# Scan inside a TensorE-bound trunk: the exponential behind the cast, y's scaling and norm sums on GpSimd, decays stored by kind, and the partition sums directly in front of the next transposes

## The chip, the cores and the metric

One core of one Trainium2 chip. The metric is the time of one execution in microseconds of device time, the median of several runs. TensorE is called PE below, VectorE DVE, ScalarE ACT, GpSimd POOL and SyncE SP, as the profile does.

## The reference, cut to what matters

One layer of a hybrid encoder on 2048 frames of 1024 columns, in float32: a norm, one input projection, a short gated convolution beside a state-space scan with 16 heads in 2 groups, an output projection over both, and an MLP. The change lies in the scan and in what follows it:

```python
x_c = xs * dt                                 # per head, 64 columns
a_cum = cumsum(dt * a_head)                   # inside a chunk
decay = exp(a_cum[l] - a_cum[s])  for l >= s  # per head, l x s
scores = C @ B.T                              # l x s, per group
y_diag = (scores * decay) @ x_c
states = B.T @ (x_c * exp(a_cum[-1] - a_cum))
h = h * exp(a_cum[-1]) + states               # carried from chunk to chunk
y_off = (C @ h_before) * exp(a_cum)
y = y_diag + y_off + d_skip * xs
gated = rmsnorm(y * silu(z))                  # over the 512 columns of a group
x = x + concat(y_a, gated) @ w_out
h = rmsnorm(x, norm_mlp_w)                    # the MLP's input
```

## The kernel before, in words

Time is cut into four blocks b of 512 frames. Every wide product is three matmuls of 128x128 by 512 on pieces of the operands (hi by hi, lo by hi, hi by lo; L114 to L116, and L271 to L273 where the products are combined in groups of seven). The in-projection of the blocks goes first, then the out-projection, then the MLP.

The scan works in 32 chunks of 128 frames: b (4) by group g (2) by c (4). A chunk n consists of:

- `load` (L1395 and on): bc (B and C), xd (x), and dec, the running sums of its 8 heads' decays, read from the HBM tensor rd_d and spread over all 128 partitions (L1411); `load_rows`: eb, the exponentials of the same sums, from the other half of rd_d; `load_gate`: the gate, into y (L1441).
- `front`: on PE four transposes ptx of x, one of B and the product C x B into ptb (L1459 to L1463); on ACT the copy xtok of ptx (L1465) and the hi casts of the pieces btok and xde (L1447), on DVE their lo parts (L1448), smask (scores under the triangle), xdt (xtok x dt, in a buffer stmp, L1471) and xtok x dend (L1473). Then, a step later, the decays: eight Relus on ACT (L1479), one Exp of 128x1024 (L1480), four scalings of xd by ACT (L1482). A step later DVE multiplies dec by smask (L1484).
- `back`: on PE st (three matmuls, new state, from btok and xde), yo (four, C by the old state, L1500) and yd (eight, dec by xdt, L1503); on DVE the state, y's sum and its gate (L1525); on ACT the squares of y (L1528), on DVE their sums over the four column tiles (L1529, L1531) into ssq. Then on PE the partition sum pss (ones by ssq, L1534, two passes), ACT's Sqrt (L1536), the reciprocal (L1537), y times it (L1539) and y's store to yn_d (L1540).

`run` is a generator, and its steps are laid between the products of the projection. The first 16 chunks (`bufs` 1, in the trace from 460 to 950 us) run beside the second half of the in-projection, a step after every 12 matmuls. The last 16 (`bufs` 2, from 950 to 1260 us) run beside the out-projection: `Output.unit` computes one column tile of one block in 24 matmuls, and its hook takes one step in the middle and two at its end. A chunk's loads are issued one chunk ahead in the first half and two ahead in the second. The unit's result is added to xt and stored (x1 in the orders, x_d in the trace; L1704, L1705), and its square is added to facc, the norm sum of the MLP's input (`Output.square`, L1716 to L1719).

The order of each engine's instructions is fixed when the program is built: a scheduler with its own estimate of times takes the instructions that are ready, in each engine's queue, with the tiles' buffers as a bound; `behind(x)` (L100) makes it put what is inside after instruction x. All DMAs here are issued by SP, in order. A DMA into a buffer waits there until the buffer's last reader is done, and so does all that is queued behind it.

Of the kernel before, what the change touches and what calls it, by code (L numbers as in the profile page):

```python
# [11 lines left out]
F32 = mybir.dt.float32  # L12
F32R = mybir.dt.float32r
AF = mybir.ActivationFunctionType
# [25 lines left out]
def trunk(ctx: ExitStack, tc: tile.TileContext, x, x_tok, w_in, w_dt, w_out, w_up, w_down, cvec, hrow, out):  # L40
# [20 lines left out]
    wide = lambda n, k: [dram.tile([P, k, TH], F32, name=f"{n}_d{h}") for h in range(2)]  # L61
    xs_d, sz_d, ys_d, yn_d = wide("xs", 12), wide("sz", 8), wide("ys", 8), wide("yn", 8)
    dt_d = [dram.tile([P, 4, NC * 16], F32, name=f"dt_d{b}") for b in range(NB)]
    rd_d = [dram.tile([NC * 16, 2, P], F32, name=f"rd_d{b}") for b in range(NB)]
    NQ = NF // 2
    hid_d = [[dram.tile([P, 7, TB], F32, name=f"hid_d{h}_{q}") for q in range(NQ)] for h in range(2)]
    sums_d = {}
# [32 lines left out]
    def behind(before):  # L100
        return tc.issue_after(before) if before is not None else nullcontext()
# [318 lines left out]
    class Proj(Seven):  # L420
# [304 lines left out]
        def dt_part(self, b):  # L725

            t = self.dt_tiles[b % NBB]
            v, e, d, p = (t[:, 64 * i : 64 * i + 64] for i in range(4))
            ct = t[:, 256:384]
            rows = t[0:64, 384:640].rearrange("p (a l) -> p a l", a=2)  # L730
            pd = psum("tp", "pd", 2)
            parts = [(k, h) for k in range(KD) for t in self.parts(b, k) for h in t]
            for n, (k, h) in enumerate(parts):
                nc.tensor.matmul(
                    pd[0:32, :], self.wdt[:, k, :], h, start=(n == 0), stop=(n == len(parts) - 1)
                )
            dts = (self.tmp("dts") if self.h == 0 else self.e("dts", TB))[0:32]
            nc.scalar.copy(dts, pd[0:32, :])
            yield
            pt = psum("tp", "pt", 2)  # L740
            for c in range(NC):
                nc.tensor.transpose(pt[:, c * 32 : (c + 1) * 32], dts[:, c * L : (c + 1) * L], ident[0:32, 0:32])
            three = lambda a: a.rearrange("p (c h) -> p c h", c=NC)
            nc.vector.tensor_reduce(
                out=three(v),
                in_=pt[:, 0 : NC * 32].rearrange("p (c s h) -> p c h s", c=NC, s=2),
                axis=mybir.AxisListType.X,
                op=ALU.add,
            )
            bias = self.hb[:, 0:16].unsqueeze(1).to_broadcast([P, NC, 16])  # L750
            nc.vector.tensor_tensor(out=three(v), in0=three(v), in1=bias, op=ALU.add)
            nc.vector.scalar_tensor_tensor(out=e, in0=v, scalar=-1.0, in1=v, op0=ALU.mult, op1=ALU.max)
            nc.scalar.activation(e, e, AF.Exp, scale=-1.0)

            nc.vector.tensor_scalar(out=d, in0=e, scalar1=2.0, scalar2=None, op0=ALU.add)
            nc.vector.reciprocal(out=d, in_=d)
            nc.vector.tensor_tensor(out=e, in0=e, in1=d, op=ALU.mult)
            nc.vector.tensor_tensor(out=d, in0=e, in1=e, op=ALU.mult)
            nc.vector.tensor_scalar(out=p, in0=d, scalar1=1.0 / 17, scalar2=None, op0=ALU.mult)
            for n in (15, 13, 11, 9, 7, 5, 3):  # L760
                nc.vector.scalar_tensor_tensor(out=p, in0=p, scalar=1.0 / n, in1=d, op0=ALU.add, op1=ALU.mult)
            nc.vector.scalar_tensor_tensor(out=p, in0=p, scalar=1.0, in1=e, op0=ALU.add, op1=ALU.mult)
            nc.vector.tensor_scalar(out=v, in0=v, scalar1=0.0, scalar2=None, op0=ALU.max)
            nc.vector.scalar_tensor_tensor(out=v, in0=p, scalar=2.0, in1=v, op0=ALU.mult, op1=ALU.add)
            nc.vector.tensor_tensor(
                out=three(e), in0=three(v), in1=self.a_neg.unsqueeze(1).to_broadcast([P, NC, 16]), op=ALU.mult
            )
            for _ in range(3 + 2 * self.h):
                yield
            pc = psum("tp", "pc", 2)  # L770
            nc.tensor.matmul(pc[:, 0:64], tri, e, start=True, stop=True)
            nc.tensor.matmul(pc[:, 64:128], ones, e, start=True, stop=True)
            nc.vector.tensor_copy(ct, pc[:, 0:128])
            nc.scalar.activation(p, ct[:, 64:128], AF.Exp)
            nc.vector.tensor_tensor(out=d, in0=ct[:, 64:128], in1=ct[:, 0:64], op=ALU.subtract)
            nc.scalar.activation(d, d, AF.Exp)
            nc.vector.tensor_tensor(out=d, in0=d, in1=v, op=ALU.mult)
            yield
            pr = psum("tp", "pr", 2)
            nc.tensor.transpose(pr[0:64, 0:P], ct[:, 0:64], ident)  # L780
            nc.vector.tensor_copy(rows[:, 0, :], pr[0:64, 0:P])
            nc.scalar.activation(rows[:, 1, :], pr[0:64, 0:P], AF.Exp)
            nc.sync.dma_start(rd_d[b], rows)
            for i, q in enumerate((v, ct[:, 0:64], p, d)):
                nc.sync.dma_start(dt_d[b][:, i], q)
            for _ in range(1 + self.h):
                yield
# [584 lines left out]
    class Scan:  # L1372
# [21 lines left out]
        def load(self, n):  # L1394

            if n >= self.end:
                return
            b, g, c, h, ts, r0 = self.place(n)
            t = self.got[n] = {}
            if (g, c) == (0, 0) or n == self.begin:  # L1400
                dd = self.tile([4, NC * 16], "dd")
                nc.sync.dma_start(dd, dt_d[b])
                self.dd = {**getattr(self, "dd", {}), b: dd}
            t["dd"] = dd = self.dd[b]
            bc = t["bc"] = self.tile([2, L], "bc", 2)
            for i in range(2):
                nc.sync.dma_start(bc[:, i], xs_d[h][:, 8 + 2 * i + g, ts])
            t["xd"] = self.tile([4, L], "xd")
            nc.sync.dma_start(t["xd"], xs_d[h][:, 4 * g : 4 * g + 4, ts])
            t["dec"] = self.tile([HG, L], "dec")  # L1410
            nc.sync.dma_start(t["dec"], rd_d[b][r0 : r0 + HG, 0, :].partition_broadcast(P))  # L1411
            three = lambda i: dd[:, i].rearrange("p (c h) -> p c h", c=NC)[:, c, g * HG : (g + 1) * HG]
            heads = lambda a: a.unsqueeze(2).to_broadcast([P, HG, 64])
            t["dt"], t["cdec"], t["dend"] = heads(three(0)), heads(three(2)), heads(three(3))
            t["a"] = dd[:, 1, r0 : r0 + HG]
            t["first"], t["last"] = (b, c) == (0, 0), (b, c) == (NB - 1, NC - 1)

        def load_rows(self, n):
# [11 lines left out]
                eb = eb[:, 0].rearrange("p (j l) -> p j l", j=4)  # L1430
            self.got[n]["eb"] = eb
            for hf in range(2):
                src = rd_d[b][r0 : r0 + HG, 1, :].rearrange("(j t) l -> t j l", t=2)[hf]
                nc.sync.dma_start(eb[hf * 64 : (hf + 1) * 64], src.partition_broadcast(64))

        def load_gate(self, n):
# [6 lines left out]
        def pieces(self, shape, tag, src):  # L1443

            pair = self.sp.tile([P] + shape, F32R, tag=tag, name=tag, bufs=1)
            hi, lo = pair[:, 0], pair[:, 1]
            nc.scalar.copy(hi, src)  # L1447
            nc.vector.tensor_tensor(out=lo, in0=src, in1=hi.bitcast(F32), op=ALU.subtract)  # L1448
            return hi, lo

        def front(self, n):
# [20 lines left out]
            if not t["last"]:  # L1472
                nc.vector.tensor_tensor(out=byhead(xtok), in0=byhead(xtok), in1=t["dend"], op=ALU.mult)  # L1473
                t["xde"] = self.pieces([2, 512], "xde", xtok)
            yield

            dec = t["dec"]
            for i in range(HG):
                nc.scalar.activation(dec[:, i], dec[:, i], AF.Relu, bias=t["a"][:, i : i + 1], scale=-1.0)  # L1479
            nc.scalar.activation(dec, dec, AF.Exp, scale=-1.0)  # L1480
            for j in range(4):
                nc.scalar.mul(t["xd"][:, j], t["xd"][:, j], col(C_D, 4 * g + j))  # L1482
            yield
# [3 lines left out]
        def back(self, n):  # L1487
# [42 lines left out]
            ssq = self.tile([L], "ssq", 1)  # L1530
            nc.vector.tensor_tensor(out=ssq, in0=q4[:, 0], in1=q4[:, 1], op=ALU.add)  # L1531
            yield
            pss = psum("tp", "pss", 2) if self.bufs == 1 else psum("mw", "pss", accs["mw"])
            nc.tensor.matmul(pss[:, 0:L], ones, ssq, start=True, stop=True)  # L1534
            r = ssq
            nc.scalar.activation(r, pss[:, 0:L], AF.Sqrt, bias=eps, scale=1.0 / 512)  # L1536
            nc.vector.reciprocal(out=r, in_=r)  # L1537
            yield
            nc.vector.tensor_tensor(out=y, in0=y, in1=r.unsqueeze(1).to_broadcast([P, 4, L]), op=ALU.mult)  # L1539
            nc.sync.dma_start(yn_d[h][:, 4 * g : 4 * g + 4, ts], y)  # L1540
            yield

        def run(self, begin, end):
# [10 lines left out]
            if self.bufs == 1:  # L1554
                for n in range(begin, end):
# [8 lines left out]
                    next(back)  # L1564
                    yield
                    yield
                    next(front, None)
                    yield
                    next(back)
                    yield  # L1570
                    next(front, None)
                    yield
# [7 lines left out]
            for n in range(begin, end):  # L1580
# [1 line left out]
                front = self.front(n + 1) if n + 1 < end else iter(())  # L1582
                next(back)
                yield
                next(before, None)
                yield
                next(back)
                self.load(n + 2)
                self.load_rows(n + 2)
                yield  # L1590
                next(front, None)
                yield
                if next(before, "end") != "end":
# [13 lines left out]
    class Output:  # L1607
# [102 lines left out]
        def square(self, b, d, t):  # L1710
# [4 lines left out]
            else:  # L1715

                sq = uh.tile([P, 1, TB], F32R, tag="ul3", name="sq", bufs=4).bitcast(F32)[:, 0]
                nc.scalar.activation(sq, t, AF.Square)
                nc.vector.tensor_tensor(out=self.accs[b], in0=sq, in1=self.accs[b], op=ALU.add)  # L1719

        def schedule(self):

# [160 lines left out]
```

## Time and profile before

| | |
|---|---|
| median of 3 runs | 2608.64 us |
| lowest, highest | 2607.66, 2610.47 us |
| the profiled execution | 2609.76 us |
| its span | 2607.8 us |
| TensorE clock granted | 0.998 |
| ScalarE busy | 1434.5 us |
| GpSimd instructions | 98 |

The profile is of one execution; 2.0 us of it lie around the span. A row of a timeline gives start, duration, engine, line, operation, output and inputs, and in brackets how long the engine sat idle before it and for whom; neighbours of one kind are put together with their count. A row of a group gives the count, the time busy, the mean duration in ns, then the idle time before. A matmul's duration in a row (0.39) is longer than its distance from the next (0.23), since they are pipelined.

### The profile page before, as it was taken

To read this page: it belongs to the slowest core of one execution; us is meant where nothing else is said; L and a number is where in the kernel's file an instruction comes from. 1 tells how busy PE (TensorE), PEld (TensorE's weight loads), DVE (VectorE), ACT (ScalarE), POOL (GpSimd) and SP (SyncE) were. 2 spreads that over 40 slices of the span, in tenths; PEclk is the share of its full clock that TensorE was granted. 3 is DMA by queue.
4 is the path that set the end of the run, shared out by engine and by line. 5 is a ranking of instruction groups with operands and counts; after the bars stand their busy time and mean duration, and the time that the engine had idled before them with its cause. 6 is when DMAs were issued, how large, how long until landed. Compare 5 with 4: busy or idle time off the path is not lost.

```text
span 2607.8 us, 33597 instructions
## 1 busy us (share of the span) xinstructions
PE 2590.0 (99%) x12067; PEld 2133.0 (82%) x12067; DVE 1909.5 (73%) x2625; ACT 1434.5 (55%) x2185; POOL 58.1 (2%) x98
## 2 busy tenths in 40 slices
PE   9999999999999999999999999999999999999998
PEld 7888888788888888887888888888888888888887
DVE  7888676777778777877767765655558877876875
ACT  7554345866667676766336555655556444444443
POOL 0000000000000000000000000000000000000001
PEclk9999999999999999999999999999999999999999
DMA  5557545545555488876665674744438766776872
GB/s 214 203 200 256 185 145 181 184 156 172 182 161 173 136 278 275 280 223 211 214 215 198 238 266 142 256 156 147 159 141 288 256 202 209 224 237 218 278 251 75
DMA packets 289558, 533.54 MB, mean 205 GB/s; under 512 B 25840, under 2 KB 141552, under 8 KB 289392
## 3 DMA queue, kind: packets, MB, share of 16 engines
q1 hardware_dynamic: 288816, 530.88, 60.4%
q8 instruction: 94, 1.54, 0.2%
q14 instruction: 72, 0.59, 0.1%
q10 hardware_dynamic: 576, 0.52, 0.1%
HBM read 354.63 MB, written 176.69 MB: 204 GB/s over the span
## 4 chain that ended last, share of the span: by engine, by line
PE 66%; issue 25%; DMA 4%; DVE 3%; ACT 2%; SPq 0%; POOL 0%; POOLq 0%; DVEq 0%; ACTq 0%
PE px L271 10%; PE px L273 10%; PE px L272 10%; PE py L271 5%; PE py L273 5%; PE py L272 5%; PE pm L114 3%; PE pm L116 3%; PE pm L115 3%; PE pw L271 2%; PE pw L272 2%; PE pw L273 2%; DMA dec<-rd_d 1%; PE pm L474 1%; PE yd L1503 1%
## 5 line engine op out<-in xcount | busy, mean ns | idle before, releaser
L271 PE MATMUL px<-uh,whi 128*128 128x512 f32 x1672 | 654.7, 392 | 2.3 <-DVE acc L1191 1.4
L272 PE MATMUL px<-ul,whi 128*128 128x512 f32 x1672 | 651.1, 389 | 0.0
L273 PE MATMUL px<-uh,wlo 128*128 128x512 f32 x1672 | 650.8, 389 | 0.0
L106 DVE TENSOR_TENSOR wlo<-wraw,whi 128x1024 fp32r<-128x1024 f32 (+2 forms) x224 | 226.5, 1011 | 203.8 <-ACT whi L105 197.8
L271 PEld LDWEIGHTS px<-uh,whi 128*128 128x128 f32 x1672 | 313.9, 188 | 72.3 <-DVE acc L1191 3.8
L273 PEld LDWEIGHTS px<-uh,wlo 128*128 128x128 f32 x1672 | 313.9, 188 | 65.8 <-issue 0.2
L272 PEld LDWEIGHTS px<-ul,whi 128*128 128x128 f32 x1672 | 314.0, 188 | 63.8
L105 ACT CAST whi<-s 128x1024 fp32r<-128x1024 f32 (+1 forms) x206 | 215.7, 1047 | 228.8 <-PE py L272 95.3
L271 PE MATMUL py<-uh,whi 128*128 128x512 f32 x836 | 326.7, 391 | 0.0
L105 ACT CAST whi<-wraw 128x1024 fp32r<-128x1024 f32 (+2 forms) x224 | 197.8, 883 | 233.9 <-PE px L272 172.2
L273 PE MATMUL py<-uh,wlo 128*128 128x512 f32 x836 | 325.4, 389 | 0.0
L272 PE MATMUL py<-ul,whi 128*128 128x512 f32 x836 | 325.4, 389 | 0.0
L106 DVE TENSOR_TENSOR wlo<-s,whi 128x1024 fp32r<-128x1024 f32 (+1 forms) x206 | 250.3, 1215 | 62.6 <-ACT whi L105 61.1
L114 PE MATMUL pm<-uh,whi 128*128 128x512 f32 (+1 forms) x584 | 226.7, 388 | 0.0
L116 PE MATMUL pm<-uh,wlo 128*128 128x512 f32 (+1 forms) x584 | 223.2, 382 | 0.0
L115 PE MATMUL pm<-ul,whi 128*128 128x512 f32 (+1 forms) x584 | 222.9, 382 | 0.0
L273 PEld LDWEIGHTS py<-uh,wlo 128*128 128x128 f32 x836 | 156.9, 188 | 32.8
L271 PEld LDWEIGHTS py<-uh,whi 128*128 128x128 f32 x836 | 156.9, 188 | 32.8 <-issue 0.5
L272 PEld LDWEIGHTS py<-ul,whi 128*128 128x128 f32 x836 | 157.0, 188 | 32.1
L327 DVE TENSOR_TENSOR ul<-rh,uh 128x1024 fp32r<-128x1024 f32 (+1 forms) x128 | 138.6, 1086 | 52.4 <-ACT uh L326 52.1
L326 ACT CAST uh<-rh 128x1024 fp32r<-128x1024 f32 (+1 forms) x128 | 120.1, 944 | 98.7 <-PE py L273 58.1
L271 PE MATMUL pw<-uh,whi 128*128 128x512 f32 x418 | 163.2, 391 | 0.0
(250 smaller groups left out, 3825.8 us busy)
## 6 DMA issues: line engine op xcount, KB each, us to landing
hid_d<-e SPq DMA_DIRECT2D x96, 512.0 KB, 4.1
rh<-hid_d SPq DMA_DIRECT2D x96, 512.0 KB, 4.8
wraw<-w_in SPq DMA_DIRECT2D x67, 512.0 KB, 3.5
wraw<-w_up SPq DMA_DIRECT2D x62, 512.0 KB, 4.0
wraw<-w_down SPq DMA_DIRECT2D x88, 256.0 KB, 4.4
dec<-rd_d SPq DMA_DIRECT2D x32, 512.0 KB, 5.0
wraw<-w_out SPq DMA_DIRECT2D x32, 512.0 KB, 4.8
x_d<-xt SPq DMA_DIRECT2D x64, 256.0 KB, 3.7
```

Of the source, the lines that this page charges most:

```text
L105: nc.scalar.copy(hi, raw)
L106: eng.tensor_tensor(out=lo, in0=raw, in1=hi.bitcast(F32), op=ALU.subtract)
L114: nc.tensor.matmul(out, whi, hi, start=(k == 0), stop=False)
L115: nc.tensor.matmul(out, whi, lo, start=False, stop=False)
L116: nc.tensor.matmul(out, wlo, hi, start=False, stop=(k == nk - 1))
L271: nc.tensor.matmul(p, hi, h[0], start=bool(first and k == 0), stop=False, **kw)
L272: nc.tensor.matmul(p, hi, h[1], start=False, stop=False, **kw)
L273: nc.tensor.matmul(p, lo, h[0], start=False, stop=(k == len(g) - 1), **kw)
L326: nc.scalar.copy(p[i][0], t)
L327: nc.vector.tensor_tensor(out=p[i][1], in0=t, in1=p[i][0].bitcast(F32), op=ALU.subtract)
L474: last[engine] = make(*args, **kw).ins
L1503: nc.tensor.matmul(yd[(i % 2) * 64 : (i % 2) * 64 + 64, (i // 2) * L : (i // 2 + 1) * L], byhead(t["xdt"])[:, i, :], t["dec"][:, i, :], st ...
```

## The change

Five edits:

- rd_d is laid out by kind: [2, 64, 128] instead of [64, 2, 128]. The 8 rows of a chunk's running sums are then 4 KB in a row, and so are the 8 rows of its exponentials; before, a row of 512 B of the one alternated with one of the other. The store (L783) and both loads follow.
- The Exp of a chunk's decays is put behind the cast xde of the same chunk, by `behind`.
- In `run`, the step of `back` that issues pss, Sqrt and reciprocal moves to directly ahead of the step of `front` that issues the next chunk's transposes. In the second half the loads of chunk n+2 also move one step earlier, into the step that follows the chunk's matmuls.
- In the first half pss takes its PSUM bank from "yo" instead of "tp".
- y times the norm (L1539, 128x512, once a chunk) and the adding up of the squares (L1719, 128x512, 14 times) go from DVE to GpSimd.

```diff
-    rd_d = [dram.tile([NC * 16, 2, P], F32, name=f"rd_d{b}") for b in range(NB)]
+    rd_d = [dram.tile([2, NC * 16, P], F32, name=f"rd_d{b}") for b in range(NB)]
...
-            nc.sync.dma_start(rd_d[b], rows)
+            nc.sync.dma_start(rd_d[b].rearrange("k r l -> r k l"), rows)
...
-            nc.sync.dma_start(t["dec"], rd_d[b][r0 : r0 + HG, 0, :].partition_broadcast(P))
+            nc.sync.dma_start(t["dec"], rd_d[b][0, r0 : r0 + HG].partition_broadcast(P))
...
-                src = rd_d[b][r0 : r0 + HG, 1, :].rearrange("(j t) l -> t j l", t=2)[hf]
+                src = rd_d[b][1, r0 : r0 + HG].rearrange("(j t) l -> t j l", t=2)[hf]
...
-            nc.scalar.copy(hi, src)
+            self.cast = nc.scalar.copy(hi, src).ins
...
                 t["xde"] = self.pieces([2, 512], "xde", xtok)
+                t["cast"] = self.cast
...
-            nc.scalar.activation(dec, dec, AF.Exp, scale=-1.0)
+            with behind(t.get("cast")):
+                nc.scalar.activation(dec, dec, AF.Exp, scale=-1.0)
...
-            pss = psum("tp", "pss", 2) if self.bufs == 1 else psum("mw", "pss", accs["mw"])
+            pss = psum("yo", "pss") if self.bufs == 1 else psum("mw", "pss", accs["mw"])
...
-            nc.vector.tensor_tensor(out=y, in0=y, in1=r.unsqueeze(1).to_broadcast([P, 4, L]), op=ALU.mult)
+            nc.gpsimd.tensor_tensor(out=y, in0=y, in1=r.unsqueeze(1).to_broadcast([P, 4, L]), op=ALU.mult)
...
                     yield
                     yield
+                    next(back)
                     next(front, None)
                     yield
-                    next(back)
                     yield
                     next(front, None)
...
                 next(back)
                 yield
-                next(before, None)
-                yield
                 next(back)
                 self.load(n + 2)
                 self.load_rows(n + 2)
                 yield
+                yield
+                next(before, None)
                 next(front, None)
                 yield
...
-                nc.vector.tensor_tensor(out=self.accs[b], in0=sq, in1=self.accs[b], op=ALU.add)
+                nc.gpsimd.tensor_tensor(out=self.accs[b], in0=sq, in1=self.accs[b], op=ALU.add)
```

Lines behind L1474 move down by one or two. Where the new order stands on PE and on ACT is shown in the prediction, beside the steps that rest on it. On SP here is the place of one load of decays, in before, second half (bc, dec and xd are the loads of chunk 26, y_9283 and y_9462 the finished y of chunks 22 and 23, xt and x1 the loads and stores of the out-projection):

```order
L1677 DMA xt_9741<-x 128x512
L1705 DMA x1_d2_79<-xt_9602 128x512
L1407 DMA bc_9782<-xs_d1_98 128x128 x2
L1411 DMA dec_9787<-rd_d3_112 128x8x128
L1677 DMA xt_9813<-x 128x512
L1409 DMA xd_9785<-xs_d1_98 128x4x128
L1434 DMA eb_10112<-rd_d3_112 64x4x128 x2
L1540 DMA yn_d1_104<-y_9462 128x4x128
```

and after the change:

```order
L1542 DMA yn_d1_104<-y_9283 128x4x128
L1707 DMA x1_d3_80<-xt_9526 128x512
L1441 DMA y_9664<-sz_d1_100 128x4x128
L1679 DMA xt_9741<-x 128x512
L1707 DMA x1_d2_79<-xt_9598 128x512
L1407 DMA bc_9764<-xs_d1_98 128x128 x2
L1411 DMA dec_9769<-rd_d3_112 128x1024
L1679 DMA xt_9813<-x 128x512
L1434 DMA eb_10108<-rd_d3_112 64x4x128
L1409 DMA xd_9767<-xs_d1_98 128x4x128
```

The store of y_9283 has moved from 9 rows ahead of these decays to 6, and that of y_9462, which stood 4 rows behind them, stands 9 behind, after the next units' xt and x1.

## The prediction

> **What bounds the kernel now.** I read the page first, then the stretches, then who waits for whom on the engine that is full, then single stretches of the timeline. The page's head and its row of busy time:
>
> ```profile
> span 2607.8 us, 33597 instructions
> PE 2590.0 (99%) x12067; PEld 2133.0 (82%) x12067; DVE 1909.5 (73%) x2625; ACT 1434.5 (55%) x2185; POOL 58.1 (2%) x98
> ```
>
> TensorE (PE) is busy all the time, so this change can give back only what the scan costs PE beside its own products; what it takes from VectorE (DVE) is worth nothing unless PE waited for it. The stretches show where idle time is. The row is the second half of the scan, which runs inside the output projection; its columns are busy time by engine, granted clock, share of the DMA engines, GB/s:
>
> ```profile
> 950.00:1260.00 310.00, 306.53 (x1643) 252.62 (x1642) 229.62 (x365) 194.69 (x387) 0.00 (x0) 1.00 0.80 248
> ```
>
> PE idles 3.5 us of these 310, the clock is full and the DMA engines are 0.80 busy. Who is waited for, from the list of waits (us in total, times, longest):
>
> ```profile
> PE st L114 <- ACT xde L1447: 2.0, 2, 1.2
> PE st L115 <- DVE xde L1448: 1.3, 4, 0.6
> ACT dec L1479 <- DMA dec<-rd_d: 51.4, 21, 6.5
> ```
>
> The first two rows are the scan's waits on PE: the state product st waits for the split of x (xde), 3.3 us. The third says why: ScalarE (ACT) waits 51.4 us for a chunk's decays to land, and the casts that st needs are queued behind that wait.
>
> **The change part by part.** One bound holds throughout: 0.2% is 5.2 us, about what a measurement of this kernel can tell from no change, so faster means under 2603.4 and slower over 2613.9.
>
> *The sum of squares (pss) in front of the transposes.* PE in before, second half, the pss of chunk 22 (pm is a product of the output projection):
>
> ```order
> L115 MATMUL pm_9528<-ul2_8455,whi_9327 128x512
> L116 MATMUL pm_9528<-uh2_8454,wlo_9328 128x512
> L1534 MATMUL pss_9586<-ssq_9488,ones_r_160 128x128
> L114 MATMUL pm_9610<-uh0_9203,whi_9327 128x512
> L115 MATMUL pm_9610<-ul0_9204,whi_9327 128x512
> ```
>
> The same pss after the change:
>
> ```order
> L116 MATMUL pm_9606<-uh0_9262,wlo_9328 128x512
> L1536 MATMUL pss_9619<-ssq_9488,ones_r_160 128x128
> L1459 MATMUL ptx_9623<-ident_155,xd_9399 128x128 x4
> L1462 MATMUL ptb_9628<-ident_155,bc_9396 128x128
> L1463 MATMUL ptb_9628<-bc_9396 128x128
> L114 MATMUL pm_9606<-uh0_9211,whi_9327 128x512
> ```
>
> It no longer stands alone between two wide products, it shares one interruption with the transposes; 27 of the 32 did stand alone. What a lone one costs, from PE's timeline (start, us):
>
> ```profile
> 1091.28 0.39 PE L116 MATMUL pm<-uh,wlo 128*128 128x512 f32 x1
> 1091.51 0.38 PE L1534 MATMUL pss<-ssq,ones_r 128*128 128x128 f32 x2
> 1091.96 0.40 PE L115 MATMUL pm<-ul,whi 128*128 128x512 f32 x1
> 1092.89 0.39 PE L116 MATMUL pm<-uh,wlo 128*128 128x512 f32 x1
> ```
>
> Four wide products take 0.93 from 1091.96 to 1092.89, 0.23 each. From 1091.28 to 1091.96 there are two of them (0.46) and the sum, so the sum costs 0.22. Its two narrow passes remain wherever they stand; only the switch between kinds of product goes. No row prices that alone; it is between nothing and a quarter of the 0.22, 0.055. I take 0.04, nearer the upper end, since the lone sum switches into the narrow form and out of it again: 27 x 0.04 = **1.1 us gained** (0 to 1.5).
>
> *The exponential behind the cast, and what now stands in front of it.* This decides. ACT in before around the transposes of chunk 24 (dec_9597 is the decays of chunk 25, one chunk ahead; ssq_9488 the norm of chunk 22; xtok, btok, xde belong to chunk 24):
>
> ```order
> L1536 ACT_TABLE_LOAD
> L1536 ACTIVATE ssq_9488<-pss_9586,cv_154 128x128
> L1479 ACTIVATE dec_9597<-dec_9597,dd_9413 128x128 x5
> L1482 ACTIVATE xd_9418<-xd_9418,cv_154 128x128
> L1465 COPY xtok_9631<-ptx_9623 128x512
> L1447 CAST btok_9633<-ptb_9628 128x128
> L1528 ACTIVATE stmp_9666<-y_9462 128x512
> L1482 ACTIVATE xd_9418<-xd_9418,cv_154 128x128 x3
> L1479 ACTIVATE dec_9597<-dec_9597,dd_9413 128x128 x2
> L1447 CAST xde_9641<-xtok_9631 128x512
> ```
>
> The same place after (dec_9593 is chunk 25's, dec_9401 chunk 24's own):
>
> ```order
> L1480 ACTIVATE dec_9593<-dec_9593,dd_9394 128x128 x3
> L1538 ACT_TABLE_LOAD
> L1538 ACTIVATE ssq_9488<-pss_9619,cv_154 128x128
> L1465 COPY xtok_9631<-ptx_9623 128x512
> L1447 CAST btok_9633<-ptb_9628 128x128
> L1484 ACTIVATE xd_9399<-xd_9399,cv_154 128x128 x3
> L1530 ACTIVATE stmp_9666<-y_9462 128x512
> L1484 ACTIVATE xd_9399<-xd_9399,cv_154 128x128
> L1480 ACTIVATE dec_9593<-dec_9593,dd_9394 128x128 x4
> L1447 CAST xde_9641<-xtok_9631 128x512
> L1482 ACT_TABLE_LOAD
> L1482 ACTIVATE dec_9401<-dec_9401 128x1024
> ```
>
> The wait for chunk 25's decays still stands in front of chunk 24's copy. The table load and Sqrt, which lay ahead of that wait, now lie behind it; and the Exp that follows the cast is of chunk 24 itself, so that the same chunk's yd, some ten us later, needs it, where before it had been done a chunk earlier. Each step's time, from ACT's timeline at this place:
>
> ```profile
> 1097.94 1.57 ACT L1479 ACTIVATE dec<-dec,dd 128x128 f32<-128x128 f32 x5 [5.64 <-DMA dec<-rd_d]
> 1099.71 0.56 ACT L1465 COPY xtok<-ptx 128x512 f32<-128x512 f32 x1
> 1100.18 0.25 ACT L1447 CAST btok<-ptb 128x128 fp32r<-128x128 f32 x1
> 1100.33 0.63 ACT L1528 ACTIVATE stmp<-y 128x512 f32<-128x512 f32 x1
> 1100.87 0.98 ACT L1482 ACTIVATE xd<-xd,cv 128x128 f32<-128x128 f32 x3
> 1102.33 0.61 ACT L1447 CAST xde<-xtok 128x512 fp32r<-128x512 f32 x1
> 1102.84 0.40 ACT L1479 ACTIVATE dec<-dec,dd 128x128 f32<-128x128 f32 x1
> 1103.15 1.04 ACT L105 CAST whi<-wraw 128x1024 fp32r<-128x1024 f32 x1
> 1105.50 1.06 ACT L1480 ACTIVATE dec<-dec 128x1024 f32<-128x1024 f32 x1
> 1106.58 1.28 ACT L1536 ACT_TABLE_LOAD   x1
> ```
>
> and two groups (busy, mean ns, then idle before):
>
> ```profile
> L1536 ACT ACTIVATE ssq<-pss,cv 128x128 f32<-128x128 f32 x32 | 11.8, 368 | 25.2 <-PE pss L1534 24.9
> L1484 DVE TENSOR_TENSOR dec<-dec,smask 128x1024 f32<-128x1024 f32 x32 | 39.0, 1218 | 1.5 <-ACT dec L1480 1.5
> ```
>
> From the landing to the first instruction of yd it is then, by starts: seven relus at 0.30, 2.1; table load and Sqrt 1.28 + 0.37; copy 0.47; btok 0.15; square 0.54; four xd 1.2; cast 0.51; table load 1.28; Exp 1.06; mask on DVE 1.22: 10.2 us. With eight relus 10.5. In before, landing to the end of the cast was 4.9 and yd hung on nothing more. What time there is, from the landings of the next chunk's decays and the yd of the chunk in hand:
>
> ```profile
> 1079.57 0.99 ACT L1479 ACTIVATE dec<-dec,dd 128x128 f32<-128x128 f32 x3 [4.80 <-DMA dec<-rd_d]
> 1087.62 1.09 PE L1503 MATMUL yd<-dec,stmp 128*64 128x128 f32 x16
> 1105.68 0.55 PE L1503 MATMUL yd<-dec,stmp 128*64 128x128 f32 x6
> 1116.92 0.99 ACT L1479 ACTIVATE dec<-dec,dd 128x128 f32<-128x128 f32 x3 [6.54 <-DMA dec<-rd_d]
> 1127.86 0.33 PE L1503 MATMUL yd<-dec,stmp 128*64 128x128 f32 x2
> 1190.90 1.28 ACT L1479 ACTIVATE dec<-dec,dd 128x128 f32<-128x128 f32 x4 [5.29 <-DMA dec<-rd_d]
> 1201.41 1.09 PE L1503 MATMUL yd<-dec,stmp 128*64 128x128 f32 x16
> 1212.65 0.99 ACT L1479 ACTIVATE dec<-dec,dd 128x128 f32<-128x128 f32 x3 [5.40 <-DMA dec<-rd_d]
> 1219.81 1.09 PE L1503 MATMUL yd<-dec,stmp 128*64 128x128 f32 x16
> ```
>
> Four of these yd (of chunks 24, 25, 29 and 30) stood behind st's waits. What one costs, at chunk 25:
>
> ```profile
> 1124.03 0.39 PE L116 MATMUL pm<-uh,wlo 128*128 128x512 f32 x1
> 1125.59 0.51 PE L114 MATMUL st<-xde,btok 128*128 128x512 f32 x1 [1.17 <-ACT xde L1447]
> 1126.31 0.50 PE L115 MATMUL st<-xde,btok 128*128 128x512 f32 x1 [0.22 <-DVE xde L1448]
> ```
>
> From 1124.03 to 1126.31 is 2.28 where two steps of 0.23 are due, so 1.8. Read in the same way the other three are 0.4, 1.5 and 0.8; together **4.5 us, which go**, since the cast now comes ahead of the Exp (the list above has 3.3 of them as idle time). Without them the chunks 23, 24, 25, 29 and 30 leave 8.1, 7.3, 9.1, 9.0 and 6.4 us. Against 10.5, 10.2, 11.5 (there a weight cast like the 1.04 of whi lies between as well), 10.5 and 10.5 yd would wait 2.4, 2.9, 2.4, 1.5 and 4.1: 13.3 us. The other chunks have over 10 us, or their copy stands ahead of the wait.
>
> *The decays by kind.* A partition's read becomes one run of 4 KB in place of eight of 512 B. Flights from the page (KB, us):
>
> ```profile
> dec<-rd_d SPq DMA_DIRECT2D x32, 512.0 KB, 5.0
> wraw<-w_out SPq DMA_DIRECT2D x32, 512.0 KB, 4.8
> wraw<-w_in SPq DMA_DIRECT2D x67, 512.0 KB, 3.5
> ```
>
> w_out is as large, in 4 KB runs, in the same stretch: 0.2 earlier; w_in, in an emptier stretch, 1.5. I take 0.5 at each of the five waits, **10.8 us of waits added** in place of 13.3; 1.5 at each leaves 5.8. The Trainium skill, in "DMA: Bandwidth & Descriptors", section Specifications, puts the least transfer for line rate at 512 B; by that the flight would not change at all and the waits would be the 13.3; the rows of w_out and dec, 0.2 apart, lean that way.
>
> *y's scaling and the norm sums on GpSimd.* From DVE go 32 and 14 instructions of 0.68; on GpSimd the only rows are these, beside DVE's neighbours in the tail:
>
> ```profile
> L1298 POOL TENSOR_TENSOR acc<-acc,rstd x9: 725/742/1507, 2581.4 to 2602.8; 128x256 f32<-128x256 f32 x6, 128x512 f32<-128x512 f32 x3
> 2580.28 0.43 DVE L1253 TENSOR_TENSOR facc<-facc,sq 128x256 f32<-128x256 f32 x1 [0.48 <-ACT sq L1251]
> 2582.99 1.23 DVE L1253 TENSOR_TENSOR facc<-facc,sq 128x256 f32<-128x256 f32 x1
> ```
>
> The 128x512 form takes up to 1.51. DVE's time is covered by PE, so nothing is gained there. y's store comes later by about 0.8, and by another 1.65 for the later Sqrt. On SP's queue, behind that store, stand x1's store, the reload of xt, bc and then the next decays: 0 to 2, I take 0.3.
>
> The sum: 10.8 + 0.3 - 4.5 - 1.1 = +5.5 on the profiled 2609.76 (span 2607.8 and 2.0 around it), 2615.3. That execution lies 1.1 above the median 2608.64 of runs from 2607.66 to 2610.47, so **2614**.
>
> **The rivals.** *The decays come in time, and the change does what it says* (faster). If each lands 2.5 us sooner (1.5 by w_in's row, and a load issued sooner because SP no longer stands behind late stores), four of the five waits are gone and the last costs 1.6; with none left 4.5 + 1.1 go: 2603, and 2602 with the switch at its upper price. It decides from 2.4 us up. Against it: the load cannot issue before the yd two chunks back has freed its buffer, and the DMA engines are at 0.80.
>
> *GpSimd stops DVE.* DVE's add took 1.23 beside GpSimd against 0.43 without it. y's scaling comes right after Sqrt and reciprocal, when DVE makes xdt and xtok x dend; where either is held, the cast and yd are later by 0.8, for both 1.6: five waits longer, 4 to 8 us, 2618 to 2622. From one hold per chunk on it shows. The Trainium skill, "SBUF — State Buffer", section Who interferes with whom, has DVE instructions with two SBUF inputs and a reading GpSimd instruction exclude each other for a whole instruction; the 1.23 agrees.
>
> *The terms cancel.* Landings 1.2 us sooner leave 7.3 of waits, of which restart and order may hide a few: 2606 to 2611, no change that can be measured.
>
> **How the numbers follow.** Forecast 0.45 (2611 to 2618; of this 0.12 below 2613.9), GpSimd 0.12, in time 0.21 (0.03 of it not past 2603.4), cancelled 0.22. So faster 0.18, same 0.12 + 0.03 + 0.22 = 0.37, slower 0.33 + 0.12 = 0.45. The range 2602 to 2622 takes in the two cases beside the forecast as priced, and leaves out what lies beyond them, by my reckoning 0.2 together; the forecast's own range is 2611 to 2618.
>
> **What would show it.** Right: in the list of waits the rows of st on xde are gone, and yd (its weight load or product) waits for dec of L1486 for some 10 us, in the second half only, at chunks 23 to 25 and 29 to 30; ACT's Exp starts after the same chunk's cast and ends within 1.5 us of that yd. For GpSimd: the products on xtok at 1.2 us or more instead of 0.68. For the faster case: dec's median flight near 3.5 and no row of yd. Wrong altogether: PE waiting anywhere outside 460 to 1260, or a pss that waits for its ssq.

## The result, and the profile after

The changed kernel takes 2633.49 us (median of 5 runs, 2631.17 to 2636.99), the kernel before 2608.64 (5 runs, 2607.66 to 2611.12): 25 us slower, and 11 us above the upper end of the predicted range. The measured ratio, which the experiments below are held against, is 1.0088, with a 95% interval of 1.0076 to 1.0101; that is 23 us (the two medians alone give 1.0095).

The page's head, after:

```profile
span 2629.4 us, 33716 instructions
PE 2595.0 (99%) x12067; PEld 2134.6 (81%) x12067; DVE 1917.8 (73%) x2579; ACT 1438.0 (55%) x2186; POOL 130.2 (5%) x144
```

The span grew by 21.6 us, with the same matmuls. 46 instructions left DVE, some 31 us of its work by the old durations, and yet DVE is busy for 8 us more. Here is where PE idles, by stretches, before (the first half of the scan):

```profile
460.00:950.00 490.00, 489.72 (x2456) 400.95 (x2455) 376.36 (x541) 345.12 (x582) 17.22 (x38) 1.00 0.54 172
```

and after (first half, and the second with the 22 us by which it grew):

```profile
460.00:950.00 490.00, 484.29 (x2418) 393.85 (x2417) 374.26 (x512) 340.67 (x572) 46.63 (x54) 1.00 0.51 167
950.00:1290.00 340.00, 325.27 (x1713) 267.63 (x1713) 242.43 (x353) 203.79 (x403) 39.51 (x28) 0.99 0.74 240
```

Idle time went from 0.3 to 5.7 us in the first half, and from 3.5 to 14.7 in the second: 16.6 of the 21.6. The other 5.0 are PE's own busy time (2590.0 to 2595.0): the products around a wait come more slowly, so that a wait, read by the starts of the products beside it, costs more than its idle time. Put product beside product in the two profiled executions, the first half ends some 9.6 us later than before and the second another 13.0; behind the scan 1.2 us come back. Who is waited for, after (idle us in total, times, longest):

```profile
PE yd L1505 <- DVE dec L1486: 6.5, 8, 1.3
PE st L114 <- ACT xde L1447: 5.4, 6, 2.2
PE px L271 <- DVE acc L1191: 2.1, 3, 1.3
PE st L115 <- DVE xde L1448: 1.9, 5, 1.0
PE pd L734 <- ACT dts L782: 1.8, 1, 1.8
PE ptx L1459 <- DMA xd<-xs_d: 1.6, 1, 1.6
```

The row of yd is there, as forecast, and the two rows of st, which were to go, have grown from 3.3 to 7.3. By starts yd's waits cost some 8 us and st's some 10, against 4.5 in all before, which is about the 13.0 of the second half. In the first half PE waits neither for yd nor for st: it waits for ACT and DVE in the in-projection's own work (dts, and px's s, buf, eb and ch) and once for a load of xd. ACT at the place that the prediction worked out, a chunk earlier (the transposes of chunk 23 start at 1089.81; dec in the first row is chunk 24's; the rows between the copy and the last three Relus are left out):

```profile
1092.27 1.58 ACT L1480 ACTIVATE dec<-dec,dd 128x128 f32<-128x128 f32 x5 [4.49 <-DMA dec<-rd_d]
1093.87 1.28 ACT L1538 ACT_TABLE_LOAD   x1
1095.17 0.37 ACT L1538 ACTIVATE ssq<-pss,cv 128x128 f32<-128x128 f32 x1
1095.43 0.58 ACT L1465 COPY xtok<-ptx 128x512 f32<-128x512 f32 x1
1097.77 0.99 ACT L1480 ACTIVATE dec<-dec,dd 128x128 f32<-128x128 f32 x3
1099.53 0.62 ACT L1447 CAST xde<-xtok 128x512 fp32r<-128x512 f32 x1 [0.77 <-DVE xtok L1473]
1100.16 1.28 ACT L1482 ACT_TABLE_LOAD   x1
1101.46 1.06 ACT L1482 ACTIVATE dec<-dec 128x1024 f32<-128x1024 f32 x1
```

The order is the forecast one: wait, Relus, table load, Sqrt, copy, cast, Exp. But the cast now waits for DVE, and here is what DVE did between (start, us; one short row ahead of the last is left out):

```profile
1095.57 0.95 DVE L1539 RECIPROCAL ssq<-ssq 128x128 f32<-128x128 f32 x1 [1.79 <-ACT ssq L1538]
1096.44 0.23 DVE L1448 TENSOR_TENSOR btok<-ptb,btok 128x128 fp32r<-128x128 f32 x1
1096.58 0.28 DVE L1469 TENSOR_TENSOR smask<-ptb,tri 128x128 f32<-128x128 f32 x1
1096.78 1.72 DVE L1471 TENSOR_TENSOR stmp<-xtok,dd 128x512 f32<-128x512 f32 x1
1098.76 0.68 DVE L1473 TENSOR_TENSOR xtok<-xtok,dd 128x512 f32<-128x512 f32 x1
```

beside GpSimd's:

```profile
1096.66 1.30 POOL L1541 TENSOR_TENSOR y<-y,ssq 128x512 f32<-128x512 f32 x1 [20.36 <-DVE ssq L1539]
```

The reciprocal releases GpSimd's scaling of y at 1096.66, 0.12 us ahead of xdt (L1471), and xdt takes 1.72 us instead of 0.68: it ends half a microsecond after GpSimd does. That is no accident of this chunk. The group of xdt, before:

```profile
L1471 DVE TENSOR_TENSOR stmp<-xtok,dd 128x512 f32<-128x512 f32 x32 | 22.0, 686 | 42.0 <-ACT xtok L1465 42.0
```

and after:

```profile
L1471 DVE TENSOR_TENSOR stmp<-xtok,dd 128x512 f32<-128x512 f32 x32 | 45.1, 1409 | 0.0
```

23 us more in 32 instructions. 26 of them overlap GpSimd's scaling of y: 24 of these are held, at a median of 1.72, and two, which start before GpSimd does, are not (0.68 and 0.63; there GpSimd's product takes 1.67 and 1.57 instead of 1.30). The six that don't overlap it keep 0.68. What PE made of it at chunk 23:

```profile
1100.20 0.49 PE L114 MATMUL st<-xde,btok 128*128 128x512 f32 x1 [1.26 <-ACT xde L1447]
1103.83 1.09 PE L1505 MATMUL yd<-dec,stmp 128*64 128x128 f32 x16 [1.28 <-DVE dec L1486]
```

From the landing at 1092.27 to yd are 11.6 us, where the prediction had 10.5. 0.77 of the difference is ACT's wait ahead of the cast, for the product that follows xdt on DVE: xdt was held for 1.04, but ACT's own work lasted until 1098.76. The rest is steps a little longer than reckoned. And st, which the Exp no longer delays, waits as well, for the same chain.

### The profile page after: what moved, and what is told of

Its sections match the earlier page's. It is cut to its first block, busy times and chain, and to the rows that moved or that the text cites. A ratio compares the mean times of both kernels' runs of the same rounds, so it can differ in the third digit from the quotient of the medians.

```text
span 2629.4 us, 33716 instructions
## 1 busy us (share of the span) xinstructions
PE 2595.0 (99%) x12067; PEld 2134.6 (81%) x12067; DVE 1917.8 (73%) x2579; ACT 1438.0 (55%) x2186; POOL 130.2 (5%) x144
## 4 chain that ended last, share of the span: by engine, by line
PE 27%; issue 24%; DMA 2%; DVE 1%; ACT 1%; POOL 0%; SPq 0%; POOLq 0%; ACTq 0%; DVEq 0%
PE px L271 4%; PE px L272 4%; PE px L273 4%; PE py L272 2%; PE py L271 2%; PE py L273 2%; PE pm L114 2%; PE pm L115 2%; PE pm L116 2%; PE pw L272 1%; PE pw L273 1%; PE pw L271 1%; DMA dec<-rd_d 1%; DMA rb<-hn_d 1%; POOL acc L1298 0%
```

## The experiments

Four theories. **S**: the moved step costs by itself, since table load, Sqrt and reciprocal now lie in the chain from the transposes to st. **G**: GpSimd holds xdt up. **E**: the Exp behind its own cast puts the mask on the path. **W**, formed later: the root is the wait for the next chunk's decays ahead of the copy, and S, G and E only lengthen a chain that this wait has already made late. All ratios are to the kernel before, measured in the same round, where its median lay between 2608.6 and 2613.9; so the expected times, which were reckoned from 2609, are compared by ratio.

### One part undone at a time

First the old step order in the changed kernel (in both halves, of which the second is shown, and with pss in its old bank):

```diff
                 next(back)
                 yield
+                next(before, None)
+                yield
                 next(back)
                 self.load(n + 2)
                 self.load_rows(n + 2)
                 yield
-                yield
-                next(before, None)
                 next(front, None)
```

> The changed kernel with the old step order (pss, Sqrt and reciprocal where they were before, the loads at their old step, pss in its old bank); the rest of the change stays. Theory S (the moved step: table load and Sqrt now stand on ACT between the decays' wait and the copy of the transposes, the reciprocal on DVE ahead of xdt, some 1.65 + 1 us longer in every chunk): nearly all of the 25 us goes, 2608 to 2615. Theory G (GpSimd's y scaling stops DVE's xdt for 1.04 us, 26 times of 32): y's scaling still runs on GpSimd, but at another time, so at most half goes, 2620 to 2630, unless the collisions go with the order. Theory E (the Exp behind its own cast puts the mask ahead of yd): 2628 or more.

Measured: 1.0004 (0.9995 to 1.0013), 22 us back. Its list of waits and xdt's group:

```profile
PE yd L1505 <- DVE dec L1486: 2.5, 3, 1.3
PE st L114 <- ACT xde L1447: 0.9, 1, 0.9
```

```profile
L1471 DVE TENSOR_TENSOR stmp<-xtok,dd 128x512 f32<-128x512 f32 x32 | 23.7, 739 | 35.5 <-ACT xtok L1465 35.5
```

GpSimd still scales y, but its work meets xdt only 3 times and holds it twice. So the steps are needed for the loss, and they bring about the collision too: S and G aren't told apart by this.

Next y's scaling and the norm sums, back on DVE:

```diff
-            nc.gpsimd.tensor_tensor(out=y, in0=y, ...)
+            nc.vector.tensor_tensor(out=y, in0=y, ...)
...
-                nc.gpsimd.tensor_tensor(out=self.accs[b], ...)
+                nc.vector.tensor_tensor(out=self.accs[b], ...)
```

> The changed kernel with y's scaling and the norm sums back on DVE. Theory G: the 1.72 us of xdt goes back to 0.68 in all chunks, the waits of PE in the first half (9.6 us) and the waits of st shrink: 2615 to 2622. Theory S: y's scaling takes 0.68 of DVE at the same place where the stop took 1.04, so 2629 to 2634. Theory E: no change, 2633.

Measured: 1.0032 (1.0019 to 1.0045): 0.0056 back, 14 us. xdt is at 0.68 in the mean, and PE idles 1.1 us in the first half instead of 5.7. Having this work on GpSimd costs that part; 8 us stay, most of them in the second half.

Next the Exp, free again:

```diff
-            with behind(t.get("cast")):
-                nc.scalar.activation(dec, dec, AF.Exp, scale=-1.0)
+            nc.scalar.activation(dec, dec, AF.Exp, scale=-1.0)
```

> The changed kernel without the order of Exp behind the cast. Theory E: the mask is done a chunk earlier again and yd's waits (6.5 us of idle time, some 8 with restarts) go, but the Exp comes back ahead of the cast in some chunks: 2623 to 2628. Theories S and G: the waits of st stay or grow, 2630 to 2638.

Measured: 1.0066 (1.0053 to 1.0078), against 1.0088: about 6 us back, where the intervals just meet. Its list has no row of yd, and st waits 12.6 us instead of 7.3. E is a cost, as the prediction had it, but the Exp behind its cast did take waits from st as well.

Last the old layout of the decays (both loads and the store as before):

```diff
-    rd_d = [dram.tile([2, NC * 16, P], F32, name=f"rd_d{b}") for b in range(NB)]
+    rd_d = [dram.tile([NC * 16, 2, P], F32, name=f"rd_d{b}") for b in range(NB)]
```

> The changed kernel with the old layout of the decays (512 B runs). All theories: the flight of dec rises by some 0.2 to 0.5 us, which the five or more chunks pay that wait for it: 2633 to 2638. If the layout by itself cost something (the store of 4 KB rows by kind), 2630 or less.

Measured: 1.0102 (1.0086 to 1.0117), against 1.0088: slower if anything, by some 4 us. The median flight of the decays is 5.3 us here and 4.9 in the changed kernel, with the same order of instructions on PE, ACT and DVE. The layout is no part of the loss.

### What the collision is, and the parts alone

xdt is taken from PSUM, so that only one of its inputs lies in SBUF:

```diff
-            nc.vector.tensor_tensor(out=byhead(t["xdt"]), in0=byhead(xtok), in1=t["dt"], op=ALU.mult)
+            nc.vector.tensor_tensor(out=byhead(t["xdt"]), in0=byhead(pt), in1=t["dt"], op=ALU.mult)
```

> The changed kernel, but xdt is made from the transposes in PSUM instead of from their copy xtok in SBUF, so that this product has one input in SBUF and not two; GpSimd's scaling of y stays where it was. Theory G (the two engines exclude each other only over DVE instructions with two inputs in SBUF): xdt takes 0.7 us and not 1.72, the first half's loss (9.6 us) falls to 1 to 4, the whole to 2617 to 2625; if GpSimd then meets the next product, xtok by dend, part of it comes back. Rival (GpSimd slows whatever DVE does beside it): xdt stays at 1.7, 2630 or more.

Measured: 1.0053 (1.0041 to 1.0065), 9 us back. The two products:

```profile
L1473 DVE TENSOR_TENSOR xtok<-xtok,dd 128x512 f32<-128x512 f32 x30 | 30.9, 1029 | 0.0
L1471 DVE TENSOR_TENSOR stmp<-ptx,dd 128x512 f32<-128x512 f32 x32 | 21.7, 677 | 0.0
```

xdt runs at its free speed with GpSimd working beside it, and now the next product, which has both inputs in SBUF, is held: 23 times, 10.5 us in all. So GpSimd does not slow whatever DVE does: in these products it holds the one with both inputs in SBUF (1.72, or 1.03 in the mean of 30, instead of 0.68), and leaves the one with an input in PSUM free (0.677). The Trainium skill ("SBUF — State Buffer", Who interferes with whom) states that a DVE instruction with two SBUF inputs contends with a GpSimd instruction that reads SBUF, and that one with at most one SBUF input, outside the 2-port modes, does not; this trace agrees with both, by the same numbers. The first half, though, still idled 4.9 us, and in the profiled execution it lost 9.2 us of the old 9.6; the expected 1 to 4 didn't come. That execution is the slowest of its six and the changed kernel's is the fastest of its five, so where the 9 us came back these two profiles don't tell, and that xdt's hold by itself makes the first half's loss is not shown.

Sqrt, and with it reciprocal and scaling, behind the cast of xde; pss stays in front of the transposes:

```diff
             nc.tensor.matmul(pss[:, 0:L], ones, ssq, start=True, stop=True)
+            yield
             r = ssq
-            nc.scalar.activation(r, pss[:, 0:L], AF.Sqrt, bias=eps, scale=1.0 / 512)
+            with behind(self.cast):
+                nc.scalar.activation(r, pss[:, 0:L], AF.Sqrt, bias=eps, scale=1.0 / 512)
```

with one more `next` for that step in each half.

> The changed kernel, pss still directly in front of the transposes on PE, but Sqrt (with its table load) and so the reciprocal and y's scaling are put behind the cast of xde on ACT. Theory S+G (the loss is Sqrt, reciprocal and y's scaling in the way of the chain from the transposes to st and yd, not the place of pss on PE): the waits of st go, xdt is back at 0.7, the first half loses under 3 us; yd still waits for the mask, since Sqrt now lies between the cast and the Exp, 6 to 9 us: 2612 to 2619. Rival (the place of pss on PE or of the loads costs): 2625 or more.

Measured: 1.0056 (1.0044 to 1.0068), 8 us back of the 23, where 14 or more were expected. st's waits went, as expected, and xdt is back at 0.74 in the mean, but yd took over, at more than twice its wait in the changed kernel:

```profile
PE yd L1505 <- DVE dec L1486: 14.6, 8, 3.2
PE st L115 <- DVE xde L1448: 0.2, 1, 0.2
```

ACT waited 86.9 us for decays here, against 68.6 in the changed kernel. With Sqrt out of the way to st the delay shows at yd instead, and the wait for the decays still stands in front of both. This is where W comes from.

The moved steps alone, on the kernel before (here the first half's; the second half's and the bank as in the change):

```diff
                     yield
                     yield
+                    next(back)
                     next(front, None)
                     yield
-                    next(back)
                     yield
```

> The kernel before with the moved steps alone (pss, Sqrt and reciprocal in front of the next transposes, loads a step earlier, the bank); scaling on DVE, old layout, Exp free. Theory S: the chain grows by table load, Sqrt and reciprocal in the second half, as with GpSimd undone: 2617 to 2624. Rival (the steps only hurt together with the Exp behind its own cast, which put the mask on the path): 2607 to 2612.

Measured: 1.0039 (1.0026 to 1.0052), 10 us. Its only large row is st's:

```profile
PE st L114 <- ACT xde L1447: 9.1, 5, 3.7
```

GpSimd alone, on the kernel before:

```diff
-            nc.vector.tensor_tensor(out=y, in0=y, ...)
+            nc.gpsimd.tensor_tensor(out=y, in0=y, ...)
...
-                nc.vector.tensor_tensor(out=self.accs[b], ...)
+                nc.gpsimd.tensor_tensor(out=self.accs[b], ...)
```

> The kernel before with y's scaling and the norm sums on GpSimd alone. Theory S+G (the collision needs the moved steps, which bring the reciprocal right ahead of xdt): xdt is held in under 6 chunks of 32, 2607 to 2614. Rival (GpSimd beside DVE costs by itself): 14 us as when it was undone, 2619 to 2625.

Measured: 1.0001 (0.9993 to 1.0010): nothing, in spite of 46 instructions that take about twice as long. xdt is held once. Steps 10, GpSimd 0, both with the rest 23: the parts do not add.

### Where the wait stands

The decays' wait moved instead: the Relus of a chunk behind the cast of the chunk ahead (with the layout by kind, all else as before):

```diff
-            nc.scalar.copy(hi, src)
+            self.cast = nc.scalar.copy(hi, src).ins
...
-            nc.scalar.copy(xtok, pt)
+            prev, self.cast = self.cast, nc.scalar.copy(xtok, pt).ins
...
-            for i in range(HG):
-                nc.scalar.activation(dec[:, i], dec[:, i], AF.Relu, ...)
+            with behind(prev):
+                for i in range(HG):
+                    nc.scalar.activation(dec[:, i], dec[:, i], AF.Relu, ...)
```

> The kernel before with the decays by kind, and the Relus of a chunk's decays put behind the cast of xde of the chunk ahead of it, so that the wait for the decays no longer stands in front of the copy of the transposes; all else as before. Theory W (that wait in front of the copy is why st waits at all): st's waits go, 4.5 us, and nothing takes their place, since Relus and Exp have some 6 us until the next transposes: 2602 to 2606, a ratio of 0.997 to 0.999. Rival (the decays land so late that the wait only moves on, to Sqrt and the next copy or to the mask): 0.9995 or more.

Measured: 0.9978 (0.9968 to 0.9988), 6 us faster than the kernel before. No row of st or yd is left in its list of PE's waits. ACT around the transposes of chunk 24 in it:

```profile
1096.65 0.69 ACT L1484 ACTIVATE xd<-xd,cv 128x128 f32<-128x128 f32 x2 [2.52 <-PE ptx L1460]
1097.24 0.57 ACT L1466 COPY xtok<-ptx 128x512 f32<-128x512 f32 x1
1099.62 0.62 ACT L1448 CAST xde<-xtok 128x512 fp32r<-128x512 f32 x1 [0.53 <-DVE xtok L1474]
1100.15 2.45 ACT L1481 ACTIVATE dec<-dec,dd 128x128 f32<-128x128 f32 x8
1104.85 1.06 ACT L1482 ACTIVATE dec<-dec 128x1024 f32<-128x1024 f32 x1
```

ACT waits for PE, not for a DMA; the eight Relus run in one piece behind the cast, with no wait at all here. In the whole kernel ACT's wait for decays fell from 51.4 us to 9.4:

```profile
ACT dec L1481 <- DMA dec<-rd_d: 9.4, 9, 1.9
```

The layout with the Exp behind its cast (the last run below) left 41.2 of it, so the layout, which is in this edit too, accounts for little. PE idles 0.2 us in the second half's old stretch (before, 3.5):

```profile
950.00:1260.00 310.00, 309.83 (x1663) 256.71 (x1662) 233.05 (x369) 197.43 (x391) 0.00 (x0) 1.00 0.79 252
```

The same edit of the Relus in the changed kernel, in place of the Exp's order; first with the scaling and the norm sums on DVE (of which the scaling is shown):

```diff
-            with behind(t.get("cast")):
-                nc.scalar.activation(dec, dec, AF.Exp, scale=-1.0)
+            nc.scalar.activation(dec, dec, AF.Exp, scale=-1.0)
...
-            nc.gpsimd.tensor_tensor(out=y, in0=y, ...)
+            nc.vector.tensor_tensor(out=y, in0=y, ...)
```

> The changed kernel with y's scaling and the norm sums back on DVE, and with the Relus behind the cast of the chunk ahead in place of the Exp behind its own. The moved steps stay: table load, Sqrt and reciprocal still lie in the chain from the transposes to st. Theory W: without the wait in front of it that chain has some 5.5 us of work for the 8 us that PE gives it, so the moved steps cost nothing more and the joined pss gives its 1 us: ratio 0.996 to 0.999. Theory S (the moved steps cost by their own length): st's waits stay, as with GpSimd undone, 1.002 to 1.005.

Measured: 0.9989 (0.9978 to 1.0000). The moved steps, which cost 10 us alone, cost nothing that can be measured here. Then the scaling and the norm sums on GpSimd:

> The same with y's scaling and the norm sums on GpSimd, as in the changed kernel. Theory W+G: xdt is held for 1.04 us in most chunks again, but in the second half the chain has the room; the first half, where no wait for decays was in front, still loses its 8 us: ratio 1.001 to 1.004. Theory S+G: 1.006 to 1.009.

Measured: 0.9998 (0.9989 to 1.0007). This kernel is the one with the Exp free (1.0066) but for the order put on eight Relus a chunk, and 18 us faster. PE's and GpSimd's instructions stand in the same order in both; around the Relus the scheduler also laid other work of ACT and DVE in another order, and that part isn't told apart. xdt is held as ever:

```profile
L1472 DVE TENSOR_TENSOR stmp<-xtok,dd 128x512 f32<-128x512 f32 x32 | 45.2, 1414 | 0.2
```

The collision is all there and costs some 2 us, not 14: 0.9998 against 0.9989, whose intervals overlap. This was less than I expected, in the first half above all. The profiled execution, 5 us above this kernel's median, has one wait of 5.8 us ahead of st, where ACT waited for another transfer in front of the cast:

```profile
1186.29 2.02 ACT L1640 ACTIVATE uh<-ry,cv 128x512 fp32r<-128x512 f32 x3 [6.49 <-DMA ry<-yn_d]
```

It is the same pattern with another load in the decays' place.

Product beside product, what the place of the Relus changes is the second half: the profiled execution of the kernel with the Exp free lost 15.6 us there against before, this one 4.6, the 5.8 us wait included; in the first half they lost 5.6 and 4.2. So W is borne out for the second half. In the first it is not told apart from the collision.

Layout and the Exp behind its cast alone, on the kernel before:

```diff
-            nc.scalar.activation(dec, dec, AF.Exp, scale=-1.0)
+            with behind(t.get("cast")):
+                nc.scalar.activation(dec, dec, AF.Exp, scale=-1.0)
```

> The kernel before with the decays by kind and the Exp behind its own cast alone; scaling on DVE, steps as before. It tells what these two are worth where Sqrt lies ahead of the wait. By the prediction's own step (the chain from landing to yd is then 1.65 shorter, 8.8 us): yd waits 1 to 3 us in all, st's 1.8 at chunk 25 goes, ratio 0.998 to 1.001. Rival (the Exp behind its cast costs as much as in the changed kernel, 6 us): 1.002 or more.

Measured: 0.9997 (0.9988 to 1.0005); yd waits 1.0 us and st 1.3. Where Sqrt lies ahead of the wait, as it does there, the Exp's order together with the layout costs nothing that can be measured; the layout alone was not run.

## Why the prediction was wrong, by its own steps

- **What bounds the kernel**: right, and the third row of the waits named the cause. The question that was not asked is what else follows from it: in the chunks where st is late already, what lies between that wait and st counts in full.
- **The exponential behind the cast**: yd's waits came, 6.5 us of idle time in 8 chunks and some 8 by starts, against 10.8 forecast; four of the five chunks named (23, 24, 29, 30) are among the eight. The mechanism was right and its size somewhat too large.
- **"4.5 us, which go"**: this is the step that failed. st's waits did not go, they grew to 7.3 us of idle time, some 10 by starts where none were forecast. I let them go because the cast comes ahead of the Exp, and did not put the table load and Sqrt, which I had just added to the chain of yd, into that of st, which is the same chain up to the cast. Where st already waited, 1.65 more for these and the reciprocal on DVE make it wait longer; the moved steps alone show it, at 9.1 us in the row that had 2.0.
- **y's scaling on GpSimd**: priced at nothing on the path, with the collision as a rival at 0.12 and 4 to 8 us. It was the other large error. The row that I quoted (1.23 against 0.43) was the right one; where the new order puts the reciprocal, right ahead of xdt, the collision is the rule, 24 holds in 32 chunks, and with the work back on DVE 14 us come back. The time of 2633 lies above that rival's 2622 too, since it left st's waits and the first half at nothing.
- **The first half at nothing**: it lost some 9.6 us. There DVE waited for Sqrt 11 times, 26.9 us, with other work queued behind, and xdt was held; what PE waited for was the in-projection's own work on ACT and DVE. With GpSimd undone PE's idle time there is 1.1 us, with the steps undone 2.6, with the Exp free 3.1, against 5.7; product beside product these three lose 1.0, 3.9 and 5.6 us there. These are single executions, and the kernels whose time is about that of before idle between 0.3 and 3.8, so how the parts share this loss stays open.
- **pss with the transposes**, 1.1 us gained: not shown. With the wait moved, the kernel with the moved steps, and so the joined pss, is no faster than the one without (0.9989 against 0.9978, overlapping).
- **The decays by kind**: the flight's median is 4.9 against 5.0, where 0.5 less was taken; undone in the changed kernel it is 5.3, and the time some 4 us longer with overlapping intervals. Right in sign, small.
- **y's later store**, 0.3 us: not seen. The decays of chunks 18 to 31 are issued in the mean 3.6 us after the first yd of the chunk two back, in both kernels.
- **The faster rival** needed the decays to land early. They didn't have to: with the place of their wait in ACT's queue moved, 6 us were gained without that. (In that rival's sum chunk 24 keeps 0.4, 2.9 less 2.5; only three of the five waits are gone. It changes nothing here.)

## What to carry to other kernels

On an engine that works in order, look for a wait on a transfer that stands ahead of work for a chunk that is already due; whatever is put behind that wait (a table load, a square root, a held product) then delays the due work by its length, while here the same work cost little or nothing once the wait stood behind the due work (0.9989 and 0.9998). Price a chain for each of its ends: what is added ahead of a fork lengthens both branches. And when work goes to GpSimd, look in the new order for what releases it, and which DVE product with both inputs in SBUF starts just behind that moment.

## What the runs showed of the hardware

The clock that PE is granted can fall behind a wait, after the work has begun again. In the changed kernel 2.17 us of idle time stand ahead of st at 1218.63. The clock is still full while st runs; from 1220 to 1223 it is 0.50, and 0.72 over these 6 us:

```profile
1218.00:1224.00 6.00, 4.63 (x28) 3.77 (x29) 4.58 (x6) 4.38 (x5) 1.78 (x1) 0.72 0.61 176
```

The eight narrow products of yo that follow take 1.83 us instead of the 1.05 that they took at chunk 23, behind a wait of 1.26 us:

```profile
1219.93 1.83 PE L1502 MATMUL yo<-bc,state 128*128 128x128 f32 x8
```

The sixteen of yd take 1.64 instead of 1.09. So this wait cost 1.3 us more than its idle time, which is a part of the 5.0 us that PE's busy time grew; it is the only place in the scan of this execution where the granted clock fell. In the run with the Relus moved and the work on GpSimd, the 8 us from 1188, in whose first microsecond the 5.8 us wait ends, had a mean clock of 0.58.
